# Three 256-column matmuls in place of one of 512 and one of 256 in the weight-stationary stages of a decoder layer

## Chip, cores and metric

The kernel runs on one core of one Trainium2 chip. The metric is the device time of one execution in microseconds; the kernel before takes 1761.91 us, the median of three runs (1760.35 to 1762.4).

## What is computed

One decoder layer for 256 tokens of width 2048, all in float32. Cut to what matters:

```
u  = x @ w_in + b_in                      # x: 256 x 2048, twelve column groups
mq, mk: causal convolution over 4 tokens, then SiLU      (16 blocks of 128 columns)
rq, rk: rotary phase                                     (16 blocks)
ga, gb: merge gates, sigmoid                             (32 blocks)
ya = headnorm(mlstm(mq, mk, mv)) * sigmoid(mo) @ w_branch_m   (16 blocks)
yb = headnorm(retention(rq, rk, rv)) * silu(rg) @ w_branch_r  (16 blocks)
y  = (sigmoid(ga) * ya + sigmoid(gb) * yb) @ w_out + b_out
x1 = layer_norm(alpha * x + y)
out = layer_norm(alpha * x1 + relu(x1 @ w1 + b1)**2 @ w2 + b2)   # w1: 2048 x 8192, 60 of 64 blocks
```

The products need more accuracy than one pass of the fast 32-bit matmul format gives, so each operand is split into a high and a low part, and a product is the sum of three: high times high, high times low, and low times high.

## The kernel before, in words

The weights are one stream of 608 groups of 128 x 1024 numbers. SyncE loads a group into a ring of four raw buffers (line 96). ScalarE rounds it to its high part `whi` (line 111), and VectorE subtracts to get the low part `wlo` (line 112). Three pairs of `whi` and `wlo` form the ring that TensorE reads; `next_w()` hands out the groups in order.

The projections are of two kinds, which alternate along the program.

*x-stationary* stages (`x_stationary`, lines 164 to 166) load 128 tokens of the activations into the array and stream 512 weight columns past them, three matmuls of 512 columns for each token half and each block of 128 input features.

*weight-stationary* stages (`w_stationary`, lines 145 and 147) load 128 x 128 weights into the array and stream the 256 tokens. A **step** is one block `kb` of 128 input features, of which there are 16; a **block** is 128 output features, so it has 16 steps and takes two weight groups. The activations `src[:, kb]` hold the high part of the 256 tokens and the low part of the 256 tokens side by side, 512 columns. There are 156 blocks: 16 for the convolution, 16 for the rotary phase, 32 for the gates, 16 for each branch, and 60 in the feed-forward part (12 in its first quarter, and 16 in each other). That is 156 x 16 = 2496 steps.

In the kernel before, a step is two matmuls. The first streams all 512 columns past `whi`, so that the left half of the PSUM bank `ps_w` gathers high times high, and the right half gathers the activations' low part times `whi`. The second streams the 256 high columns past `wlo` and adds to the left half. When the block ends, its consumer has two partial sums to add: ScalarE copies the right half to a tile `t` in SBUF, and VectorE adds it to the left half. There are four PSUM buffers for these sums.

Between steps, `step()` lets a background list of small work go on: the attention-like heads (`m_head`, `r_head`) and transposes (`to_pair`). The heads call `exact` (lines 375 to 377), which is also a run of three matmuls per term; in `r_head` these have 256 columns each, and each has its own weights. A scheduler fixes the order of instructions on each engine when the program is built; an engine runs its list in order.

Of the kernel before, what the change touches and what calls it, by code (L numbers as in the profile page):

```python
# [10 lines left out]
F32 = mybir.dt.float32  # L11
F32R = mybir.dt.float32r
I32 = mybir.dt.int32
AF = mybir.ActivationFunctionType
OP = mybir.AluOpType
PSUM = bass.MemoryType.PSUM

P = 128
T = 256
D = 2048  # L20
KB = D // P
# [13 lines left out]
C_BIN, C_CW, C_CB, C_MG, C_RG, C_BF, C_INVF, C_SIGN, C_LG, C_LB, NCOL = 0, 64, 128, 144, 160, 176, 240, 241, 242, 258, 274  # L35
# [4 lines left out]
def layer_kernel(ctx: ExitStack, tc: tile.TileContext, xT, x, pos, wp, wg, cols, rows, b_in, b_ff1, gbias,  # L40
                 cst, decay, sel, out):
    nc = tc.nc
    V, S, TE, G = nc.vector, nc.scalar, nc.tensor, nc.gpsimd
# [5 lines left out]
    wk = ctx.enter_context(tc.tile_pool(name="wk", bufs=2))  # L49
    sm = ctx.enter_context(tc.tile_pool(name="sm", bufs=4))  # L50
    pmm = ctx.enter_context(tc.tile_pool(name="pmm", bufs=4, space=PSUM))
    pat = ctx.enter_context(tc.tile_pool(name="pat", bufs=4, space=PSUM))

    def big(name):
        return s16.tile([P, 4096], F32, tag="s16", name=name)

    def pair(name):
        return t32.tile([P, KB, 2, T], F32R, tag="t32", name=name)

# [1 line left out]
    NG = wp.shape[0]  # L61
    RAW_B, HL_B = 4, 3
    raws, parts, place = {}, {}, {}
# [55 lines left out]
    def step():  # L119
        while bg:  # L120
            try:
                next(bg[0])
                return
            except StopIteration:
                bg.pop(0)
# [5 lines left out]
    def next_w():  # L131
        g = state["use"]
        split_until(g + HL_B)
        state["use"] += 1
        return parts.pop(g)

    def w_stationary(src, n_blocks, consume):
        for blk in range(n_blocks):
            ps = pmm.tile([P, 512], F32, tag="mm", name="ps_w")
            for g in range(KB // 8):  # L140
                hi, lo = next_w()
                for j in range(8):
                    kb = g * 8 + j
                    c = slice(j * P, (j + 1) * P)
                    TE.matmul(ps, hi[:, c], src[:, kb].rearrange("p a t -> p (a t)"),  # L145
                              start=kb == 0, stop=False)
                    TE.matmul(ps[:, :T], lo[:, c], src[:, kb, 0], start=False, stop=kb == KB - 1)  # L147
                if g == 0:
                    step()
            consume(blk, ps)  # L150
            step()
# [46 lines left out]
        return ([(g, h) for h in range(2) for g in range(HOLD)],  # L198
                [(g, h) for g in range(HOLD, n) for h in range(2)])

# [1 line left out]
    xraw = big("xraw").rearrange("p (k t) -> p k t", k=KB)  # L202
    xs = pair("xs")
    warm = cp.tile([P, 1], F32, name="warm")
# [8 lines left out]
    col = cp.tile([P, NCOL], F32, name="col")  # L213
# [16 lines left out]
    def rows_bc(dst, i):  # L230
        nc.sync.dma_start(dst, bass.AP(tensor=rows.tensor, offset=rows.offset + i * D, ap=[[0, P], [1, D]]))

# [1 line left out]
    ex = cp.tile([P, MH, 384], F32, name="ex")  # L234
    em = cp.tile([P, 2, MH], F32, name="em")
    cos_t = cp.tile([P, T], F32, name="cos_t")
# [119 lines left out]
        yield  # L356
        V.tensor_scalar(sin_t, sin_t, col[:, C_SIGN:C_SIGN + 1], None, OP.mult)

# [1 line left out]
    def rstd_of(dst, var, n):  # L360
        v = sm.tile([P, n], F32, tag=f"ve{n}", name="ve")
        V.tensor_scalar(v, var, EPS, None, OP.add)
# [119 lines left out]
                V.scalar_tensor_tensor(dst[:, eb + i, 1], t, g, dst[:, eb + i, 0].bitcast(F32),  # L482
                                       OP.mult, OP.subtract)

# [1 line left out]
    def halves(t):  # L486
        return t.rearrange("p (a b) -> p a b", a=2)

# [29 lines left out]
    mqk = big("mqk").rearrange("p (k t) -> p k t", k=16)  # L518

    def conv_silu(blk, ps):  # L520
        t = wk.tile([P, T], F32, tag="t1", name="t1")
        S.activation(t, ps[:, T:], AF.Copy)
        zp = wk.tile([P, T + 4], F32, tag="zp", name="zp")
        V.memset(zp[:, 0:4], 0.0)
        V.scalar_tensor_tensor(zp[:, 4:], ps[:, :T], col[:, C_BIN + blk:C_BIN + blk + 1], t, OP.add, OP.add)
        y = wk.tile([P, T], F32, tag="y", name="y")
        V.tensor_scalar(y, zp[:, 1:1 + T], col[:, C_CW + blk:C_CW + blk + 1],
                        col[:, C_CB + blk:C_CB + blk + 1], OP.mult, OP.add)
        for k in range(1, CONV_K):
            c = C_CW + 16 * k + blk  # L530
            V.scalar_tensor_tensor(y, zp[:, 1 + k:1 + k + T], col[:, c:c + 1], y, OP.mult, OP.add)
        sg = wk.tile([P, T], F32, tag="sg", name="sg")
        S.activation(sg, y, AF.Sigmoid)
        V.scalar_tensor_tensor(mqk[:, blk], y, MDQK ** -0.5 if blk < 8 else 1.0, sg, OP.mult, OP.mult)
# [10 lines left out]

    x_stationary(xs, KB, 4, mo_chunk)

# [1 line left out]
    hmT = []  # L549
    rqk = big("rqk").rearrange("p (k t) -> p k t", k=16)  # L550

    def rotary(blk, ps):
        t = wk.tile([P, T], F32, tag="t1", name="t1")
        S.activation(t, ps[:, T:], AF.Copy)
        z = wk.tile([P, T], F32, tag="y", name="y")
        V.scalar_tensor_tensor(z, ps[:, :T], col[:, C_BIN + 16 + blk:C_BIN + 17 + blk], t, OP.add, OP.add)
        w = wk.tile([P, T], F32, tag="sg", name="sg")
        S.copy(w[0:64], z[64:128])
        S.copy(w[64:128], z[0:64])
        V.tensor_tensor(z, z, cos_t, OP.mult)  # L560
        V.tensor_tensor(w, w, sin_t, OP.mult)
        V.tensor_tensor(rqk[:, blk], z, w, OP.add)
        if blk == 3:
            bg.append(to_pair(mo_t, hmT, C_MG, 0, 16))
# [12 lines left out]

    x_stationary(xs, KB, 4, rg_chunk)

# [1 line left out]
    def gate(dst, c0):  # L581
        def consume(blk, ps):
            t = wk.tile([P, T], F32, tag="t1", name="t1")
            S.activation(t, ps[:, T:], AF.Copy)
            V.tensor_tensor(t, ps[:, :T], t, OP.add)
            S.activation(dst[:, blk], t, AF.Sigmoid, bias=col[:, c0 + blk:c0 + blk + 1])
        return consume

    drain_bg()
    sga = big("sga").rearrange("p (k t) -> p k t", k=16)  # L590
    w_stationary(xs, 16, gate(sga, C_BIN + 32))
    sgb = big("sgb").rearrange("p (k t) -> p k t", k=16)
    w_stationary(xs, 16, gate(sgb, C_BIN + 48))

# [1 line left out]
    hrT = []  # L596

    def branch_m(blk, ps):
        t = wk.tile([P, T], F32, tag="t1", name="t1")
        S.activation(t, ps[:, T:], AF.Copy)  # L600
        V.tensor_tensor(t, ps[:, :T], t, OP.add)
        V.tensor_tensor(sga[:, blk], sga[:, blk], t, OP.mult)

    bg.append(to_pair(rg_t, hrT, C_RG, 0, 16))
    w_stationary(hmT[0], 16, branch_m)
# [6 lines left out]
    mgT = pair("mgT")  # L612

    def branch_r(blk, ps):
        t = wk.tile([P, T], F32, tag="t1", name="t1")
        S.activation(t, ps[:, T:], AF.Copy)
        V.tensor_tensor(t, ps[:, :T], t, OP.add)
        y = wk.tile([P, T], F32, tag="y", name="y")
        V.tensor_tensor(y, sgb[:, blk], t, OP.mult)
        V.tensor_tensor(y, sga[:, blk], y, OP.add)  # L620
        S.copy(mgT[:, blk, 0], y)
        V.tensor_tensor(mgT[:, blk, 1], y, mgT[:, blk, 0].bitcast(F32), OP.subtract)
        if blk in (4, 8):
            half = blk // 4 - 1
            V.scalar_tensor_tensor(xr[:, half], xr[:, half], ALPHA, bob, OP.mult, OP.add)

    w_stationary(hrT[0], 16, branch_r)

# [1 line left out]
    hold(G_OUT + 24 + 8 - HOLD, [(s16, 2), (s16, 2), (s16, 2)])  # L630
    hold(G_FF, [(s16, 2), (s16, 2), (s16, 2)])
    st1 = sm.tile([P, 2, 4, 6], F32, tag="st1", name="st1", bufs=2)
# [48 lines left out]

    x_split(mgT, *late(KB), first_norm)

# [1 line left out]
    hT = pair("hT")  # L685
    brow = wk.tile([P, 512], F32, tag="brow", name="brow")
    nc.sync.dma_start(brow, bass.AP(tensor=b_ff1.tensor, offset=b_ff1.offset, ap=[[0, P], [1, 512]]))
# [18 lines left out]
    b2 = big("b2")[:, 0:D]  # L706
# [14 lines left out]
    for q in range(4):  # L721
        if q:
            hT = pair("hT")

        def up(blk, ps, q=q, hT=hT):
            blk += 4 if q == 0 else 0
            t = wk.tile([P, T], F32, tag="t1", name="t1")
            S.activation(t, ps[:, T:], AF.Copy)
            V.tensor_tensor(t, ps[:, :T], t, OP.add)
            c = C_BF + q * 16 + blk  # L730
            rl = wk.tile([P, T], F32, tag="sg", name="sg")
            S.activation(rl, t, AF.Relu, bias=col[:, c:c + 1])
            y = wk.tile([P, T], F32, tag="y", name="y")
            V.tensor_tensor(y, rl, rl, OP.mult)
            S.copy(hT[:, blk, 0], y)
            V.tensor_tensor(hT[:, blk, 1], y, hT[:, blk, 0].bitcast(F32), OP.subtract)
            if q == 0 and blk in (9, 10, 11, 12):
                skip_rows(blk - 9)

        w_stationary(x1T, 16 if q else 12, up)  # L740
        if q == 3:
            hold(G_FF + 4 * 64 - HOLD, [(s16, 2), (t32, 4)])

        def down(c, ps, q=q):
            for half in range(2):
                if q < 3:
                    o = xr[:, half, c * 512:(c + 1) * 512]
                    V.tensor_tensor(o, ps[half], o, OP.add)
                else:
                    add_half(c, half, ps[half], st2)  # L750

        x_stationary(hT, KB, 4 if q < 3 else 3, down)
# [16 lines left out]
    x_split(hT, *late(KB), second_norm)  # L769


# [1 line left out]
def _stat(w):  # L773
    k, n = w.shape
    return w.reshape(k // P // 8, 8, P, n // P, P).transpose(3, 0, 2, 1, 4).reshape(-1, P, GW)
# [27 lines left out]
def _lay_out(i):  # L803
    w_in, b_in = np.asarray(i["w_in"])[0], np.asarray(i["b_in"])[0]
    w1, w2 = np.asarray(i["w_ff1"])[0], np.asarray(i["w_ff2"])[0]
    c = lambda o, n: w_in[:, o:o + n]  # noqa: E731
    parts = [_move(c(O_MV, D)), _stat(c(O_MQ, D)), _move(c(O_MO, D)), _stat(c(O_RQ, D)), _move(c(O_RV, D)),
             _move(c(O_RG, D)), _stat(c(O_GA, 2 * D)), _stat(np.asarray(i["w_branch_m"])[0]),
             _stat(np.asarray(i["w_branch_r"])[0]), _move(np.asarray(i["w_out"])[0])]
# [4 lines left out]
    wp = np.concatenate(parts, axis=0)  # L814
    x = np.asarray(i["x"])[0]
    cst, dec, sel, fc = _constants()
    b2 = lambda v: np.asarray(v).reshape(-1, P).T  # noqa: E731
    cols = np.concatenate([
        b2(b_in[O_MQ:O_MQ + D]), b2(b_in[O_RQ:O_RQ + D]), b2(b_in[O_GA:O_GA + 2 * D]),
        *[b2(np.asarray(i["m_conv_w"])[0][k]) for k in range(CONV_K)], b2(np.asarray(i["m_conv_b"])[0]),  # L820
# [23 lines left out]
```

## Time and profile before

| | before |
|---|---|
| median of three runs | 1761.91 us |
| span of the profiled execution, first to last instruction | 1760.6 us |
| TensorE (PE) busy | 1740.9 us, 99%, 8882 matmuls and 8882 weight loads |
| VectorE (DVE) busy | 1111.0 us, 63% |
| ScalarE (ACT) busy | 840.7 us, 48% |
| granted TensorE clock | 0.998 of full speed |

The profiled execution's span lies 1.3 us under the median of the timed runs; that difference is taken as what lies around the span. Matmuls overlap in the pipeline, so that a row's duration is longer than the time it takes from the stream. What a matmul costs is the distance from its start to the start of the next one, its **pitch** in what follows.

### The profile page before, as it was taken

The page shows a single profiled execution, that of the slowest core. Times are in us where ns is not written, and L with a number is a line of the kernel's source. Part 1 is how long each engine was busy: PE and PEld are TensorE (multiplying, and loading weights), DVE is VectorE, ACT ScalarE, POOL GpSimd, SP SyncE. Part 2 cuts the span into 40 slices and gives each one's busy share as a digit, 9 for nine tenths or more (in the row PEclk, how much of TensorE's full clock was granted, in tenths as well). Part 3 has the DMA queues.
Part 4 walks back from the last instruction along what each step waited for, and adds up shares of the span by engine and source line. Part 5 has one row for each costly group of instructions (what it writes and reads, how often), then busy time and mean ns, then how long its engine had stood idle before and what let it go on. Part 6 is the DMA issues. An engine that isn't in the chain of part 4 may idle for free.

```text
span 1760.6 us, 23131 instructions
## 1 busy us (share of the span) xinstructions
PE 1740.9 (99%) x8882; PEld 1475.3 (84%) x8882; DVE 1111.0 (63%) x1535; ACT 840.7 (48%) x1144; POOL 19.7 (1%) x24
## 2 busy tenths in 40 slices
PE   8999999999999999999999999999999999999997
PEld 6888888888888888888888878888888888888885
DVE  5788766875566645466666578655665566556656
ACT  5454444654444544554444465534553455345532
POOL 0000000000000000000000000000000000000001
PEclk9999999999999999999999999999999999999999
DMA  8565545456665456555555557555555555555553
GB/s 288 177 205 188 194 166 167 168 191 203 205 206 187 163 183 238 184 193 189 188 186 189 199 186 280 192 192 192 184 188 194 191 189 187 195 191 183 189 193 130
DMA packets 96439, 339.44 MB, mean 193 GB/s; under 512 B 10820, under 2 KB 12868, under 8 KB 95304
## 3 DMA queue, kind: packets, MB, share of 16 engines
q1 hardware_dynamic: 96328, 337.97, 56.7%
q8 instruction: 69, 1.13, 0.2%
q14 instruction: 42, 0.34, 0.1%
HBM read 335.83 MB, written 2.10 MB: 192 GB/s over the span
## 4 chain that ended last, share of the span: by engine, by line
PE 58%; issue 40%; DVE 1%; POOL 0%; ACT 0%; DMA 0%; SPq 0%; POOLq 0%; ACTq 0%
PE ps_w L145 20%; PE ps_w L147 10%; PE ps_x L164 8%; PE ps_x L165 8%; PE ps_x L166 8%; PE tp L475 0%; PE n L375 0%; PE ps_x L187 0%; PE ps_x L186 0%; PE ps_x L185 0%; PE n L376 0%; PE n L377 0%; PE gp L247 0%; PE sp L382 0%; DVE xr L766 0%
## 5 line engine op out<-in xcount | busy, mean ns | idle before, releaser
L112 DVE TENSOR_TENSOR wlo<-raw,whi 128x1024 fp32r<-128x1024 f32 (+1 forms) x593 | 722.7, 1219 | 545.3 <-ACT whi L111 541.8
L111 ACT CAST whi<-raw 128x1024 fp32r<-128x1024 f32 (+1 forms) x593 | 619.8, 1045 | 706.1 <-PE ps_x L165 377.2
L145 PE MATMUL ps_w<-xs,whi 128*128 128x512 f32 x1024 | 363.4, 399 | 0.0
L145 PE MATMUL ps_w<-x1T,whi 128*128 128x512 f32 x960 | 338.1, 397 | 0.0
L147 PE MATMUL ps_w<-xs,wlo 128*128 128x256 f32 x1024 | 287.6, 281 | 0.0
L147 PE MATMUL ps_w<-x1T,wlo 128*128 128x256 f32 x960 | 269.5, 281 | 0.0
L145 PEld LDWEIGHTS ps_w<-xs,whi 128*128 128x128 f32 x1024 | 192.4, 188 | 47.0
L145 PEld LDWEIGHTS ps_w<-x1T,whi 128*128 128x128 f32 x960 | 180.2, 188 | 43.9
L164 PE MATMUL ps_x<-whi,xs 128*128 128x512 f32 x512 | 201.8, 394 | 4.9 <-ACT whi L111 4.9
L165 PE MATMUL ps_x<-whi,xs 128*128 128x512 f32 x512 | 200.6, 392 | 0.0
L166 PE MATMUL ps_x<-wlo,xs 128*128 128x512 f32 x512 | 200.1, 391 | 0.0
L147 PEld LDWEIGHTS ps_w<-xs,wlo 128*128 128x128 f32 x1024 | 193.5, 189 | 0.1
L165 PE MATMUL ps_x<-whi,hT 128*128 128x512 f32 x480 | 186.8, 389 | 0.0
L164 PE MATMUL ps_x<-whi,hT 128*128 128x512 f32 x480 | 186.8, 389 | 0.0
L166 PE MATMUL ps_x<-wlo,hT 128*128 128x512 f32 x480 | 186.7, 389 | 0.0
L145 PE MATMUL ps_w<-yT,whi 128*128 128x512 f32 x512 | 181.8, 400 | 0.0
L147 PEld LDWEIGHTS ps_w<-x1T,wlo 128*128 128x128 f32 x960 | 181.4, 189 | 0.2
L147 PE MATMUL ps_w<-yT,wlo 128*128 128x256 f32 x512 | 143.8, 281 | 0.0
L164 PEld LDWEIGHTS ps_x<-whi,xs 128*128 128x128 f32 x512 | 96.8, 189 | 25.5 <-ACT whi L111 5.0
L145 PEld LDWEIGHTS ps_w<-yT,whi 128*128 128x128 f32 x512 | 96.2, 188 | 23.5
L166 PEld LDWEIGHTS ps_x<-wlo,xs 128*128 128x128 f32 x512 | 96.8, 189 | 20.6 <-DVE wlo L112 0.2
L165 PEld LDWEIGHTS ps_x<-whi,xs 128*128 128x128 f32 x512 | 96.9, 189 | 19.7
(246 smaller groups left out, 1546.5 us busy)
## 6 DMA issues: line engine op xcount, KB each, us to landing
raw<-in_wp SPq DMA_DIRECT2D x601, 512.0 KB, 3.4
brow<-in_b_in SPq DMA_DIRECT2D x16, 256.0 KB, 4.4
gb<-in_rows SPq DMA_DIRECT2D x4, 1024.0 KB, 8.2
raw<-in_wp SPq DMA_DIRECT2D x14, 256.0 KB, 4.6
xraw<-in_xT SPq DMA_DIRECT2D x8, 256.0 KB, 6.5
xr<-in_x SPq DMA_DIRECT2D x1, 2048.0 KB
dec<-in_decay SPq DMA_DIRECT2D x8, 192.0 KB, 3.1
bob<-in_rows SPq DMA_DIRECT2D x1, 1024.0 KB, 5.4
```

Of the source, the lines that this page charges most:

```text
L111: S.copy(hi[:, c], r[:, c])
L112: V.tensor_tensor(lo[:, c], r[:, c], hi[:, c].bitcast(F32), OP.subtract)
L145: TE.matmul(ps, hi[:, c], src[:, kb].rearrange("p a t -> p (a t)"), start=kb == 0, stop=False)
L147: TE.matmul(ps[:, :T], lo[:, c], src[:, kb, 0], start=False, stop=kb == KB - 1)
L164: TE.matmul(ps[half], src[:, kb, 0, t], hi[:, w], start=first, stop=False)
L165: TE.matmul(ps[half], src[:, kb, 1, t], hi[:, w], start=False, stop=False)
L166: TE.matmul(ps[half], src[:, kb, 0, t], lo[:, w], start=False, stop=last)
```

## The change

A step of `w_stationary` becomes three matmuls of 256 columns: `whi` with the high columns, `whi` with the low columns, `wlo` with the high columns. All three add to the same 256 columns of PSUM, so the finished sum stands there when the block ends. The tile `t`, the copy to it, and the addition go away in all six consumers; ScalarE (or VectorE, in the branches) reads the sum from PSUM, and adds the bias on the way.

```diff
     def w_stationary(src, n_blocks, consume):
         for blk in range(n_blocks):
-            ps = pmm.tile([P, 512], F32, tag="mm", name="ps_w")
+            ps = pmm.tile([P, T], F32, tag="mm", name="ps_w")
...
-                    TE.matmul(ps, hi[:, c], src[:, kb].rearrange("p a t -> p (a t)"),
-                              start=kb == 0, stop=False)
-                    TE.matmul(ps[:, :T], lo[:, c], src[:, kb, 0], start=False, stop=kb == KB - 1)
+                    TE.matmul(ps, hi[:, c], src[:, kb, 0], start=kb == 0, stop=False)
+                    TE.matmul(ps, hi[:, c], src[:, kb, 1], start=False, stop=False)
+                    TE.matmul(ps, lo[:, c], src[:, kb, 0], start=False, stop=kb == KB - 1)
...
     def conv_silu(blk, ps):
-        t = wk.tile([P, T], F32, tag="t1", name="t1")
-        S.activation(t, ps[:, T:], AF.Copy)
         zp = wk.tile([P, T + 4], F32, tag="zp", name="zp")
         V.memset(zp[:, 0:4], 0.0)
-        V.scalar_tensor_tensor(zp[:, 4:], ps[:, :T], col[:, C_BIN + blk:C_BIN + blk + 1], t, OP.add, OP.add)
+        S.activation(zp[:, 4:], ps, AF.Identity, bias=col[:, C_BIN + blk:C_BIN + blk + 1])
...
         def consume(blk, ps):
-            t = wk.tile([P, T], F32, tag="t1", name="t1")
-            S.activation(t, ps[:, T:], AF.Copy)
-            V.tensor_tensor(t, ps[:, :T], t, OP.add)
-            S.activation(dst[:, blk], t, AF.Sigmoid, bias=col[:, c0 + blk:c0 + blk + 1])
+            S.activation(dst[:, blk], ps, AF.Sigmoid, bias=col[:, c0 + blk:c0 + blk + 1])
...
     def branch_m(blk, ps):
-        t = wk.tile([P, T], F32, tag="t1", name="t1")
-        S.activation(t, ps[:, T:], AF.Copy)
-        V.tensor_tensor(t, ps[:, :T], t, OP.add)
-        V.tensor_tensor(sga[:, blk], sga[:, blk], t, OP.mult)
+        V.tensor_tensor(sga[:, blk], ps, sga[:, blk], OP.mult)
...
         def up(blk, ps, q=q, hT=hT):
             blk += 4 if q == 0 else 0
-            t = wk.tile([P, T], F32, tag="t1", name="t1")
-            S.activation(t, ps[:, T:], AF.Copy)
-            V.tensor_tensor(t, ps[:, :T], t, OP.add)
             c = C_BF + q * 16 + blk
             rl = wk.tile([P, T], F32, tag="sg", name="sg")
-            S.activation(rl, t, AF.Relu, bias=col[:, c:c + 1])
+            S.activation(rl, ps, AF.Relu, bias=col[:, c:c + 1])
```

`rotary` changes as `conv_silu` does, and `branch_r` as `branch_m` does.

How the lists of the engines change is seen at two places. On TensorE, where the first weight-stationary stage (the convolution's) follows an x-stationary one, the list before reads:

```order
L166 MATMUL ps_x<-wlo,xs 128x512
L145 MATMUL ps_w<-xs,whi 128x512
L147 MATMUL ps_w<-xs,wlo 128x256
L145 MATMUL ps_w<-xs,whi 128x512
L147 MATMUL ps_w<-xs,wlo 128x256
L145 MATMUL ps_w<-xs,whi 128x512
L147 MATMUL ps_w<-xs,wlo 128x256
```

and now, with the activations `xs` streamed and `whi` or `wlo` loaded:

```order
L166 MATMUL ps_x<-wlo,xs 128x512
L145 MATMUL ps_w<-xs,whi 128x256
L146 MATMUL ps_w<-xs,whi 128x256
L147 MATMUL ps_w<-xs,wlo 128x256
L145 MATMUL ps_w<-xs,whi 128x256
L146 MATMUL ps_w<-xs,whi 128x256
L147 MATMUL ps_w<-xs,wlo 128x256
```

Three steps stood in these rows, and two stand there now; the columns streamed in a step stay 768, the matmuls go from two to three, and nothing else moves on TensorE.

On ScalarE, in the middle of the convolution's stage, the list before reads (`t` is the copied right half, `sg` the sigmoid of the convolved block, `whi` the rounding of the next weight groups):

```order
L111 CAST whi<-raw 128x1024 x2
L533 ACTIVATE sg<-y 128x256
L522 ACTIVATE t_1366<-ps_w 128x256
L111 CAST whi<-raw 128x1024 x2
L533 ACTIVATE sg<-y 128x256
L522 ACTIVATE t_1424<-ps_w 128x256
```

and now:

```order
L111 CAST whi<-raw 128x1024
L523 ACTIVATE zp<-ps_w,col 128x256
L111 CAST whi<-raw 128x1024
L531 ACTIVATE sg<-y 128x256
L111 CAST whi<-raw 128x1024
L523 ACTIVATE zp<-ps_w,col 128x256
```

The sigmoid, which waits for VectorE, has moved from behind both roundings of a block to between them; the instruction that reads the block's sum stands at the same distance in roundings as before.

## Rows read from the trace of the kernel before

**Rows 1.** The page's head, and the busy time of each engine:

```profile
span 1760.6 us, 23131 instructions
PE 1740.9 (99%) x8882; PEld 1475.3 (84%) x8882; DVE 1111.0 (63%) x1535; ACT 840.7 (48%) x1144; POOL 19.7 (1%) x24
```

**Rows 2.** Chain that ended last, shares of the span by engine:

```profile
PE 58%; issue 40%; DVE 1%; POOL 0%; ACT 0%; DMA 0%; SPq 0%; POOLq 0%; ACTq 0%
```

**Rows 3.** Waits of PE: total us, times, longest us:

```profile
PE ps_x L164 <- ACT whi L111: 4.9, 1, 4.9
PE ps_x L187 <- DVE ve L362: 1.4, 1, 1.4
PE tp L667 <- ACT xr L664: 0.5, 1, 0.5
```

**Rows 4.** PE groups by line and shape: count, busy us, mean ns, idle before:

```profile
L145 PE MATMUL ps_w<-xs,whi 128*128 128x512 f32 x1024 | 363.4, 399 | 0.0
L145 PE MATMUL ps_w<-x1T,whi 128*128 128x512 f32 x960 | 338.1, 397 | 0.0
L145 PE MATMUL ps_w<-yT,whi 128*128 128x512 f32 x512 | 181.8, 400 | 0.0
```

**Rows 5.** Busy time by engine in an x-stationary, then a weight-stationary stage:

```profile
1306.20:1393.10 86.90, 86.90 (x386) 71.97 (x385) 44.73 (x43) 34.73 (x35) 0.00 (x0) 1.00 0.57 194
1215.80:1306.10 90.30, 90.30 (x512) 78.36 (x511) 56.19 (x79) 48.35 (x77) 0.00 (x0) 1.00 0.54 187
```

**Rows 6.** Timeline of PE, three weight-stationary steps: start us, duration us:

```profile
1250.05 0.40 PE L145 MATMUL ps_w<-x1T,whi 128*128 128x512 f32 x1
1250.29 0.28 PE L147 MATMUL ps_w<-x1T,wlo 128*128 128x256 f32 x1
...
1251.11 0.40 PE L145 MATMUL ps_w<-x1T,whi 128*128 128x512 f32 x1
```

**Rows 7.** Timeline of PE, three x-stationary matmuls and the first step behind them:

```profile
102.07 0.39 PE L164 MATMUL ps_x<-whi,xs 128*128 128x512 f32 x1
...
102.75 0.39 PE L145 MATMUL ps_w<-xs,whi 128*128 128x512 f32 x1
```

**Rows 8.** Timeline of PE, a head's nine 256-column matmuls inside an x-stationary stage:

```profile
505.53 0.28 PE L375 MATMUL n<-rv,ph 128*128 128x256 f32 x1
505.65 0.28 PE L376 MATMUL n<-rv,pl 128*128 128x256 f32 x1
...
506.59 0.40 PE L164 MATMUL ps_x<-whi,xs 128*128 128x512 f32 x1
```

**Rows 9.** Timeline of the weight loads (PEld) of the same run:

```profile
505.54 0.19 PEld L376 LDWEIGHTS n<-rv,pl 128*128 128x128 f32 x1
```

**Rows 10.** Timeline of PE, the same run of a later head, inside a weight-stationary stage:

```profile
580.24 0.28 PE L377 MATMUL n<-rv,ph 128*128 128x256 f32 x1
...
581.03 0.28 PE L147 MATMUL ps_w<-xs,wlo 128*128 128x256 f32 x1
581.15 0.40 PE L145 MATMUL ps_w<-xs,whi 128*128 128x512 f32 x1
```

**Rows 11.** Timeline of PE, eleven steps in the feed-forward part's first quarter:

```profile
1090.11 0.28 PE L147 MATMUL ps_w<-x1T,wlo 128*128 128x256 f32 x1
...
1093.93 0.28 PE L147 MATMUL ps_w<-x1T,wlo 128*128 128x256 f32 x1
```

**Rows 12.** Instructions on the tile `t`: ns min/median/max, first and last start:

```profile
L728 ACT ACTIVATE t<-ps_w x60: 369/377/386, 1068.7 to 1662.3; 128x256 f32<-128x256 f32 x60
L729 DVE TENSOR_TENSOR t<-ps_w,t x60: 415/417/425, 1069.1 to 1663.6; 128x256 f32<-128x256 f32 x60
L525 DVE SCALAR_TENSOR_TENSOR zp<-ps_w,col,t x16: 475/476/479, 110.7 to 195.9; 128x256 f32<-128x256 f32 x16
```

**Rows 13.** The page's groups of the split: busy us, mean ns, idle before:

```profile
L112 DVE TENSOR_TENSOR wlo<-raw,whi 128x1024 fp32r<-128x1024 f32 (+1 forms) x593 | 722.7, 1219 | 545.3 <-ACT whi L111 541.8
L111 ACT CAST whi<-raw 128x1024 fp32r<-128x1024 f32 (+1 forms) x593 | 619.8, 1045 | 706.1 <-PE ps_x L165 377.2
```

More of the change, by code (lines that the diff above doesn't have):

```diff
@@ L552, in rotary @@
     def rotary(blk, ps):
-        t = wk.tile([P, T], F32, tag="t1", name="t1")
-        S.activation(t, ps[:, T:], AF.Copy)
         z = wk.tile([P, T], F32, tag="y", name="y")
-        V.scalar_tensor_tensor(z, ps[:, :T], col[:, C_BIN + 16 + blk:C_BIN + 17 + blk], t, OP.add, OP.add)
+        S.activation(z, ps, AF.Identity, bias=col[:, C_BIN + 16 + blk:C_BIN + 17 + blk])
         w = wk.tile([P, T], F32, tag="sg", name="sg")
@@ L614, in branch_r @@
     def branch_r(blk, ps):
-        t = wk.tile([P, T], F32, tag="t1", name="t1")
-        S.activation(t, ps[:, T:], AF.Copy)
-        V.tensor_tensor(t, ps[:, :T], t, OP.add)
         y = wk.tile([P, T], F32, tag="y", name="y")
-        V.tensor_tensor(y, sgb[:, blk], t, OP.mult)
+        V.tensor_tensor(y, ps, sgb[:, blk], OP.mult)
         V.tensor_tensor(y, sga[:, blk], y, OP.add)
@@ L726, in up @@
             blk += 4 if q == 0 else 0
-            t = wk.tile([P, T], F32, tag="t1", name="t1")
-            S.activation(t, ps[:, T:], AF.Copy)
-            V.tensor_tensor(t, ps[:, :T], t, OP.add)
             c = C_BF + q * 16 + blk
             rl = wk.tile([P, T], F32, tag="sg", name="sg")
-            S.activation(rl, t, AF.Relu, bias=col[:, c:c + 1])
+            S.activation(rl, ps, AF.Relu, bias=col[:, c:c + 1])
             y = wk.tile([P, T], F32, tag="y", name="y")
```

## The prediction

> **What bounds the kernel now.** I read four views, in this order. The page's head first: TensorE is busy 99% of a span of 1760.6 us, VectorE 63%, ScalarE 48% [rows 1]. A busy TensorE need not be a full one, so the chain that ended last comes next. It gives TensorE 58% and "issue" 40%, and nearly nothing to any other engine [rows 2]: the end is set by matmuls that follow one another, not by a wait for a consumer. The waits of TensorE agree: 4.9 us once at the start, then 1.4 and 0.5 us [rows 3], and no idle time at all ahead of the three groups of line 145 [rows 4]. So the time of a weight-stationary stage is its number of steps times the time that TensorE takes for one, and the rest of this prediction is about that time.
>
> For it I leave the durations, which overlap, and take starts. In a steady weight-stationary stage three steps take 1251.11 − 1250.05 = 1.06 us, so one takes **353.3 ns** [rows 6]; the stage's window says the same, 90.30 us for 512 matmuls, 256 steps [rows 5]. In the feed-forward part's first quarter eleven steps take 3.82 us, so one takes 347.3 ns there [rows 11]. An x-stationary matmul of 512 columns takes (102.75 − 102.07)/3 = 226.7 ns [rows 7]. Those stages are not touched by the change, and are the yardstick for what 512 columns cost.
>
> There are 1024 + 960 + 512 = 2496 steps [rows 4]. 192 of them, 12 blocks, lie in the first quarter. A nanosecond for each step is 2.5 us, or 0.14% of the time. That is the scale of everything below.
>
> **The change part by part.**
>
> *Consumers.* The copy to `t` takes 0.37 us of ScalarE, and the addition 0.42 or 0.48 us of VectorE [rows 12]. Over 156 blocks that is up to 156 × 0.377 = 59 us less on ScalarE, of which 32 copies stay (convolution and rotary turn the copy into one that adds the bias), so some 47 us; and 124 × 0.417 + 32 × 0.477 = 67 us less on VectorE. I cost this at nothing. What hides it is TensorE: it does not wait for these engines in these stages [rows 3, 4]. A gain is bounded by TensorE's waits, which lie elsewhere: the 4.9 us at the start and the 1.4 us come in front of x-stationary work. A loss would need ScalarE to be late with the roundings. They have 706.1 us of idle time in front of them, more than half of it waiting for TensorE to free a ring buffer [rows 13]. In the convolution's stage the sigmoid now stands between the two roundings of a block, so the second one waits behind it for VectorE's chain (some five operations of 0.4 to 0.5 us, and one or two `wlo` subtractions of 1.2 us, 4 to 5 us in all [rows 12, 13]); a block takes 16 × 0.353 = 5.65 us and the ring holds three groups, half a block each. I take nothing here too; if the cover were gone, sixteen blocks late by 0.5 us would be 8 us.
>
> *Matmuls.* Columns stay at 768 for each step. One more weight load and one more matmul come in: 2496 each, 28% more than the 8882 of before. Does the pair of `whi` matmuls share one load? The trace counts as many loads as matmuls [rows 1], so I take three loads for a step.
>
> What three 256-column matmuls, each with its own load, cost in a row, the trace shows in the heads' runs. In the first, which begins behind steady x-stationary work as most weight-stationary stages do, nine matmuls take 506.59 − 505.53 = 1.06 us, **117.8 ns** each [rows 8]. Their loads start with them: the load of the second starts 0.01 us after the first matmul [rows 9], so a load is hidden behind one 256-column matmul, though with nothing to spare. Three times 117.8 is 353.3 ns. That is the time of the step of before: 2304 columns take 1.06 us in both [rows 6, 8].
>
> In a later head's run, inside a weight-stationary stage, seven matmuls take 581.03 − 580.24 = 0.79 us, 112.9 ns each; by 226.7/2 it would be 113.3, so this is the yardstick's rate without any loss [rows 7, 10]. Three would be 340 ns, 13.3 less than now. But the first matmul of the stage's own operands behind it takes 0.12 us again [rows 10].
>
> So the new step has two prices from rows, 340 and 353.3 ns. I take 353.3: it is the rate on entry from x-stationary work, held for all nine matmuls, and the cheaper sequence stopped as soon as the operands of a weight-stationary stage came.
>
> *Sum.* 2304 steps at 353.3 − 353.3 = 0; the 192 of the first quarter at 353.3 − 347.3 = 6 ns more, 1.2 us; consumers 0. 1760.6 + 1.2 = 1761.8 us of span. The median lies 1.3 us above the span shown, so **1763 us**, which is no change that can be measured. Its own range is 1759 to 1767.
>
> The Trainium skill ("TensorE: Matmul & The Clock Gate", section "Back-to-back issue gap") gives a gap of N/2.4 + 2.5 ns at the full clock. That is 216 + 109 = 325 ns for the old step and 328 for the new, so 2.5 ns a step, an estimate of 6 us more. The trace does not agree with its level: 353.3 ns for the old step [rows 6].
>
> **The rivals.**
>
> *Slower: a fixed cost for each matmul.* A 512-column matmul takes 226.7 ns in an x-stationary stage, and two of 256 columns 2 × 117.8 = 235.6 [rows 7, 8]: cutting one in two costs 8.9 ns. If a weight-stationary step loses its present 353.3 − (226.7 + 117.8) = 8.8 ns for another reason, such as the roles of the two operands, then the cut adds its 8.9 on top: 362.2 ns, 2496 × 8.9 = 22 us, **1784 us**. It decides as soon as the step exceeds 354.8 ns, 0.2% of the time. For it speaks that three loads must now each hide behind a 256-column matmul; against it, that the nine matmuls of the first head carried three loads in every 353.3 ns [rows 8]. They were only nine, and a stage has 768 or more; the trace shows no longer run. The section of the Trainium skill just named is this rival's rule, a fixed part for each matmul; the trace agrees that there is one, but not with 2.5 ns.
>
> *Faster in part.* The cheaper rate [rows 10] is taken up wherever a head or a burst of transposes has broken the rhythm, and then held. Such stages are the rotary one, the gates and branches, which follow one another, and the first quarter: 16 + 64 blocks, 1280 steps at 13.3 ns, and 192 at 7.3. That is 17.0 + 1.4 = 18 us less, **1744 us**. For it: the first quarter does run at another rate, 347.3 ns, from its start's disturbance to its end [rows 11], so a rhythm once found can be kept. Against: the 0.12 us at the end of that sequence [rows 10].
>
> *Faster throughout.* The stall belongs to the mix of 512 and 256 columns, and equal matmuls run at 113.3 ns: 2304 × 13.3 + 1.4 = 32 us less, **1730 us**. Against it stand the nine matmuls at 117.8 ns [rows 8].
>
> **How the numbers follow.** No change 0.42, slower 0.23, faster in part 0.23, faster throughout 0.12. A measurement of this kernel tells 0.2%, 3.5 us, from no change (its three runs lie within 0.12%). The likeliest case is 1763. The range goes down to 1741, which takes in the partly faster case and leaves out the full one, 0.12; and up to 1781, which takes in a fixed cost of up to 8 ns a step and leaves out the rest, some 0.08.
>
> **What would show it.** In the profile after, TensorE has 11378 matmuls and as many loads. Three starts of line 145 in a row in a weight-stationary stage lie 1.06 us apart; 1.02 us would show the cheaper rate, 1.09 the fixed cost. The same window question by stage tells whether stages differ. TensorE shows no idle time ahead of the groups of `ps_w`; if it does, and ends it on line 111 or 112, the consumers' new order was wrongly costed at nothing. VectorE's busy time falls by some 67 us, ScalarE's by some 40 to 50, with no effect on the span. The prediction is wrong if the short sequences of the heads do not stand for a stage of several hundred equal matmuls, in either direction.

## The result, and the profile after

The changed kernel takes **1780.53 us** (median of 4 runs, 1780.24 to 1781.86) beside 1762.16 us for the kernel before on the same chip: a ratio of **1.0103**, 95% interval 1.0091 to 1.0116. It is slower by 18 us. (Two later executions enter no comparison: one of the kernel called e2 below, 2471.45 us, and the first of e5, 3525.67 us, which ran at half pace from end to end, though its trace lists a granted clock of 1.000, and was repeated.)

The page's head and busy times, which answer to [rows 1]:

```profile
span 1778.5 us, 27765 instructions
PE 1758.8 (99%) x11378; PEld 1609.0 (90%) x11378; DVE 1056.8 (59%) x1379; ACT 810.0 (46%) x1020; POOL 19.2 (1%) x24
```

11378 matmuls and as many loads: every matmul brings its own. VectorE has 54 us less to do and ScalarE 31 us, and the span has grown by 17.9 us all the same. The chain that ended last has not changed its kind [rows 2]:

```profile
PE 58%; issue 40%; DVE 1%; POOL 0%; DMA 0%; ACT 0%; POOLq 0%
```

Nor have the waits of TensorE (total us, times, longest us); as in [rows 3], none stands ahead of a `ps_w`:

```profile
PE ps_x L164 <- ACT whi L111: 5.3, 1, 5.3
PE ps_x L187 <- DVE ve L362: 1.4, 1, 1.4
PE tp L654 <- ACT xr L651: 0.5, 1, 0.5
```

So the 17.9 us lie in the matmuls themselves. Busy time by engine in the second quarter's two stages, the weight-stationary one first; the columns are the window, its length, then PE, PEld, DVE, ACT and POOL with their counts, the granted clock, DMA share and GB/s:

```profile
1228.50:1320.60 92.10, 92.10 (x769) 92.06 (x769) 51.56 (x64) 43.78 (x62) 0.00 (x0) 1.00 0.54 184
1320.70:1407.50 86.80, 86.80 (x385) 71.91 (x384) 44.02 (x41) 34.42 (x34) 0.00 (x0) 1.00 0.57 194
```

(A window's count takes in a matmul that hangs over its edge.) The x-stationary stage is what it was, 86.8 us beside 86.9 [rows 5]. The weight-stationary one, 768 matmuls or 256 steps, went from 90.3 to 92.1 us: 120.0 ns a matmul and 360 ns a step, at the same granted clock. The timeline of PE inside it (start us, duration us), which answers to [rows 6]:

```profile
1250.14 0.28 PE L145 MATMUL ps_w<-x1T,whi 128*128 128x256 f32 x1
1250.26 0.28 PE L146 MATMUL ps_w<-x1T,whi 128*128 128x256 f32 x1
1250.38 0.28 PE L147 MATMUL ps_w<-x1T,wlo 128*128 128x256 f32 x1
1250.50 0.28 PE L145 MATMUL ps_w<-x1T,whi 128*128 128x256 f32 x1
...
1251.10 0.28 PE L147 MATMUL ps_w<-x1T,wlo 128*128 128x256 f32 x1
```

0.12 us each, without exception, where the prediction had hoped for 0.1178. That pace holds in all weight-stationary stages, the first quarter's too:

```profile
1080.00:1140.00 60.00, 60.00 (x502) 60.00 (x501) 39.02 (x54) 29.24 (x42) 0.00 (x0) 1.00 0.61 205
```

2304 steps at 360 − 353.3 = 6.7 ns and 192 at 360 − 347.3 = 12.7 ns [rows 6, 11] are 15.4 + 2.4 = 17.8 us: the whole of the difference in the spans.

### The profile page after: what moved, and what is told of

The parts are those of the page before. It is cut to its first block, busy times and chain, and to the rows that moved or that the text cites. A ratio compares the mean times of both kernels' runs of the same rounds, so it can differ in the third digit from the quotient of the medians.

```text
span 1778.5 us, 27765 instructions
## 1 busy us (share of the span) xinstructions
PE 1758.8 (99%) x11378; PEld 1609.0 (90%) x11378; DVE 1056.8 (59%) x1379; ACT 810.0 (46%) x1020; POOL 19.2 (1%) x24
## 4 chain that ended last, share of the span: by engine, by line
PE 58%; issue 40%; DVE 1%; POOL 0%; DMA 0%; ACT 0%; POOLq 0%
PE ps_w L146 10%; PE ps_w L147 10%; PE ps_w L145 10%; PE ps_x L164 8%; PE ps_x L165 8%; PE ps_x L166 8%; PE tp L475 0%; PE ps_x L187 0%; PE ps_x L185 0%; PE ps_x L186 0%; PE n L375 0%; PE n L376 0%; PE n L377 0%; PE gp L247 0%; PE sp L382 0%
## 5 line engine op out<-in xcount | busy, mean ns | idle before, releaser
L145 PE MATMUL ps_w<-xs,whi 128*128 128x256 f32 x1024 | 290.6, 284 | 0.0
L146 PE MATMUL ps_w<-xs,whi 128*128 128x256 f32 x1024 | 289.7, 283 | 0.0
L146 PE MATMUL ps_w<-x1T,whi 128*128 128x256 f32 x960 | 271.8, 283 | 0.0
L145 PE MATMUL ps_w<-x1T,whi 128*128 128x256 f32 x960 | 271.7, 283 | 0.0
L146 PEld LDWEIGHTS ps_w<-xs,whi 128*128 128x128 f32 x1024 | 196.5, 192 | 0.1
L145 PEld LDWEIGHTS ps_w<-xs,whi 128*128 128x128 f32 x1024 | 196.5, 192 | 0.1
L145 PEld LDWEIGHTS ps_w<-x1T,whi 128*128 128x128 f32 x960 | 184.3, 192 | 0.2
L146 PEld LDWEIGHTS ps_w<-x1T,whi 128*128 128x128 f32 x960 | 184.3, 192 | 0.2
L145 PE MATMUL ps_w<-yT,whi 128*128 128x256 f32 x512 | 145.5, 284 | 0.0
```

Source lines behind the costliest of these rows:

```text
L145: TE.matmul(ps, hi[:, c], src[:, kb, 0], start=kb == 0, stop=False)
L146: TE.matmul(ps, hi[:, c], src[:, kb, 1], start=False, stop=False)
```

## The experiments

A pitch is read below as a window's length divided by its matmuls; in a window of 60 us the matmuls that hang over its edges make it up to 0.6 ns too low. e3 to e8 were executed once each, so that their whole times tell little; their stages are what is read.

### Which half of the change costs it

e1 has the three matmuls, but lets the low activations' product into the right half of the region, and keeps the old consumers. Against the kernel before:

```
-  TE.matmul(ps, hi[:, c], src[:, kb].rearrange("p a t -> p (a t)"), start=kb == 0, stop=False)
+  TE.matmul(ps[:, :T], hi[:, c], src[:, kb, 0], start=kb == 0, stop=False)
+  TE.matmul(ps[:, T:], hi[:, c], src[:, kb, 1], start=False, stop=False)
```

> Three 256-column matmuls for each step, but the low-part product goes to the right half of the bank as before, and the consumers of before copy and add. If the whole 18 us come from the matmuls: 1780 us, steps of 360 ns. If part of it comes from the consumers' new order on ScalarE: clearly under 1780, down to 1762 if all does.

Measured: 1779.89 us, ratio 1.0098 (1.0084 to 1.0112). e2 has the old matmuls and the new consumers, which read the left half alone (`consume(blk, ps[:, :T])`).

> The two matmuls of before, with the changed consumers, which read only the left half of the bank; the addition of the right half (low part of the activations times high part of the weights) is left out. If the matmuls carry the loss: 1762 us, steps of 353 ns. If the consumers carry a part of it: over 1765.

Measured: 1762.67 us, ratio 0.9999 (0.9990 to 1.0009), with VectorE at 1056.9 us and ScalarE at 810.4 us as in the changed kernel. The matmuls are the whole loss, and the 85 us of busy time taken off the two other engines are worth nothing.

### A fixed cost for each matmul, or a load that is too long?

e3 gives each stage its own number of columns n (the three matmuls of a step then take the columns `[:n]`, `[512 - n:]` and `[:n]`; the first matmul of a block keeps at least 256).

> As the changed kernel, but in all but the first of a block's 16 steps the three matmuls stream another number of columns in each stage: 288 in the convolution's, 224 and 192 in the gates', 320 and 240 in the branches', 384, 128 and 160 in the feed-forward quarters two to four; 256 stays in the rotary one and the first quarter. Tokens beyond are left out, or low-part columns taken in their place. Only the start-to-start time in each stage is read. Theory A, the load sets it: a weight load can't be ready for the next matmul sooner than 120 ns after the start of this one; then 128 to 256 columns all take 120 ns, and 288, 320 and 384 take the streaming rate of 512 columns, 0.4427 ns each: 127.5, 141.7 and 170.0. Theory B, a fixed cost of 6.7 ns for each matmul beside that rate: 63, 78, 92, 106, 113, 120, 134, 148 and 177 ns for 128, 160, 192, 224, 240, 256, 288, 320 and 384.

Windows of stages (same columns as above) with 128, 192, 240, 256, 288 and 384 columns:

```profile
1466.20:1551.90 85.70, 85.70 (x769) 85.70 (x767) 51.34 (x64) 43.68 (x62) 0.00 (x0) 1.00 0.61 197
690.00:760.00 70.00, 70.00 (x628) 70.00 (x628) 31.87 (x26) 32.33 (x40) 0.00 (x0) 1.00 0.66 227
895.00:965.00 70.00, 70.00 (x624) 70.00 (x623) 47.28 (x65) 31.46 (x40) 0.00 (x0) 1.00 0.60 196
1088.80:1158.80 70.00, 70.00 (x585) 69.94 (x584) 48.26 (x65) 33.93 (x48) 0.00 (x0) 1.00 0.66 226
103.60:205.00 101.40, 101.40 (x769) 101.40 (x768) 73.96 (x125) 47.72 (x65) 0.00 (x0) 1.00 0.51 169
1245.90:1378.90 133.00, 133.00 (x768) 132.96 (x768) 51.58 (x64) 45.33 (x62) 0.00 (x0) 1.00 0.39 128
```

The pitches are 111.6, 111.5, 112.2, 119.9, 132.0 and 173.2 ns. Half as many columns still cost 111.6: up to 240 columns something else than the stream sets the pace. PEld, busy all the time, suggests the load; narrower loads beside such short streams were not tried, so that is not shown. By the yardstick of 226.7 ns for 512 columns [rows 7] the streams of the last three would take 113.3, 127.5 and 170.0; they lose 6.6, 4.5 and 3.2 ns (and the stage with 320 columns, whose starts lie 147 ns apart, some 5). Neither theory came out: the floor is near 111.5, not 120, and the loss is no constant. It is greatest where the stream is just longer than the floor. (The Trainium skill, "TensorE: Matmul & The Clock Gate", section "LDWEIGHTS (loading the stationary operand)", gives a load columns/1.2 ns, by which an estimate for 128 columns is 107 ns; the floor of 111.6 ns lies some 4% above it.)

e4 leaves the stream alone and narrows the loads: `hi[:, c][:, :m]` into `ps[:m]`, m by stage.

> As the changed kernel, but in all but the first and last of a block's 16 steps the weight loads have fewer columns in some stages (the other output features are left out): 96 for all three in the convolution's stage, 64 in the second gate's, 32 in the second branch's; in the feed-forward quarters two to four 128, 128 and 64; 128, 64 and 64; 96, 64 and 96. All matmuls stream 256 columns. Theory A, the load sets the time: with 96 columns or fewer all fall to 113.3 ns, and in a mixed step only the matmul during which a 128-column load runs stays at 120. Theory B, a fixed cost for each matmul: 120 ns everywhere.

The stages with all loads 64, 96 and 32 wide:

```profile
700.00:750.00 50.00, 50.00 (x440) 50.00 (x439) 22.07 (x18) 22.69 (x28) 0.00 (x0) 1.00 0.58 190
110.00:190.00 80.00, 80.00 (x691) 80.00 (x690) 64.73 (x115) 42.26 (x59) 0.00 (x0) 1.00 0.57 190
860.00:940.00 80.00, 80.00 (x690) 75.25 (x689) 52.15 (x71) 34.63 (x43) 0.00 (x0) 1.00 0.58 190
```

113.6, 115.8 and 115.9 ns, beside 120.0 with loads of 128: the streams are the same, and most of the loss goes when the loads get narrower. It does not fall in step with the width, so it isn't simply the load's length. Nor does it belong to one matmul alone. Stages with loads of 128, 128 and 64 in a step, then of 128, 64 and 64:

```profile
1230.00:1300.00 70.00, 70.00 (x601) 70.00 (x600) 40.10 (x50) 34.72 (x51) 0.00 (x0) 1.00 0.59 188
1400.00:1480.00 80.00, 80.00 (x681) 80.00 (x679) 45.55 (x57) 38.89 (x56) 0.00 (x0) 1.00 0.58 187
```

They come to 116.5 and 117.5 ns in the mean, where theory A's 120.0 beside each load of 128 would give 117.8 and 115.5: the second narrow load makes it dearer. A narrow load also means a narrow output here, so e4 alone does not tell the two apart; the runs that follow, which move the streamed or the loaded tile and leave the output's width alone, speak for the load.

### What load and stream have to do with each other

They read the same memory. Three kernels move tiles there, by an unused tile of 32 bytes at the head of everything (e6), or of 32 (e7) or 64 bytes (e8) between the weights and all that follows, the activations first:

```
e6   cp.tile([P, 8], F32, name="pad")
e7   t32.tile([P, 8], F32, tag="pad", name="pad", bufs=1)
e8   t32.tile([P, 16], F32, tag="pad", name="pad", bufs=1)
```

> The changed kernel, with 32 bytes put ahead of the weight ring, so that all that follows starts 32 bytes later, on a multiple of 128 bytes. If the extra time over 113.3 ns comes from reads that straddle a line: 113 ns a matmul, 1745 to 1748 us. If it is a matter of the load beside the stream alone: 120 ns, 1780 us.

> The changed kernel, with 32 bytes put between the weight ring and the activations: weights stay where they were, activations start on a multiple of 128 bytes. If loads and streams collide by their relative place in a line: another time than 120 ns a matmul, between 113 and 127. If not: 120 ns, 1780 us.

> The same with 64 bytes. If the relative place in a line matters, another time than with 0 and 32 bytes; if not, 120 ns and 1780 us.

e6, 1779.54 us; a weight-stationary stage:

```profile
1228.50:1320.60 92.10, 92.10 (x767) 92.01 (x767) 50.87 (x63) 43.59 (x63) 0.00 (x0) 1.00 0.56 183
```

e7, 1780.32 us; the convolution's stage, then an x-stationary one:

```profile
106.20:195.70 89.50, 89.50 (x769) 89.50 (x768) 71.64 (x125) 47.77 (x65) 0.00 (x0) 1.00 0.58 192
1139.60:1229.00 89.40, 89.40 (x386) 72.00 (x385) 44.34 (x41) 34.32 (x34) 0.00 (x0) 1.00 0.56 189
```

e8, 1775.05 us; the convolution's stage, the second gate stage, an x-stationary one:

```profile
104.70:195.00 90.30, 90.30 (x768) 90.29 (x767) 71.64 (x125) 47.81 (x65) 0.00 (x0) 1.00 0.56 190
690.00:750.00 60.00, 60.00 (x532) 60.00 (x531) 26.97 (x22) 27.28 (x34) 0.00 (x0) 1.00 0.60 197
1131.70:1221.10 89.40, 89.40 (x386) 71.66 (x385) 44.34 (x41) 34.19 (x34) 0.00 (x0) 1.00 0.57 188
```

Moving everything changes nothing. Moving the activations against the weights changes every pitch: at 32 bytes 256 columns fall from 120.0 to 116.5 ns, at 64 bytes to 117.6 and, in the stages between 328 and 797 us of the span, to 113. In both, 512 columns of the x-stationary stages, where the activations are the loaded tile, rise from 226 to 232.8 ns, which takes most or all of it back; so the whole time hides what the stages show. What counts is the **distance** between the streamed and the loaded tile. In the memory map of the changed kernel, and of the one before, the streamed activations `xs`, `yT` and `x1T` and all six weight buffers leave the same remainder by 512 bytes (`xs` at 70496, the first `whi` at 45920), and the slices that a matmul takes of them begin on multiples of 512 bytes: distance 0. The heads' operands, from which the prediction took its price, do not: `rv` lies 448 bytes beyond a multiple of 512 from `ph`, since the two `zp` buffers ahead of `ph` are no multiple of 512 long.

e5 varies within a step which weights and activations meet, at distance 0: the low weights second, the high weights three times, the high activations three times, the old 512-column matmul for two steps and then two low parts ("pairs"), and an x-stationary stage cut into 256 columns.

> As the changed kernel, with one thing varied in each stage. Convolution and third feed-forward quarter: the low weights come second, so that no load repeats the one before. Second gate and fourth quarter: the third matmul takes the high weights too, so that all three loads of a step are the same (leaves out the low part of the weights). Second branch: all three stream the high columns (leaves out the activations' low part). Second quarter: the 512-column matmul of before, with the two 256-column ones of two steps behind each other (its right half is not added). Retention values, an x-stationary stage: each 512-column matmul cut into two of 256, the activations still loaded and the weights streamed. If the 120 ns come from a 128-column load that runs beside a 256-column stream, whatever the operands: 120 ns in all of these but the second quarter. If repeated loads or the one ring buffer that is read twice matter: 113 or 118 ns in the convolution's stage. If the roles of the operands matter: 113 ns in the cut x-stationary stage. The second quarter: 353 ns a step if only the mean count of 256-column matmuls matters, up to 347 to 360 otherwise.

What is read comes from a second execution of the same kernel:

> The changed kernel, whose first execution of this form ran at half the TensorE clock throughout and so told nothing; again as one look. Stages differ in the three matmuls of a step, and some leave out or change part of the sum: the conv and third up stages issue the low weights second (same sum); the second gate stage and the fourth up stage use the high weights three times; the second branch stage uses the high activations three times; the second up stage streams 512 columns twice for a pair of steps and then the two low parts; the retention values' weight-moving stage is cut from 512 to 256 columns. The rest is as changed. Theory A (the 120.0 ns come from what one matmul's stream and the next one's load touch in SBUF at the same time): 120.0 ns in the plain stages, another figure by at least 1 ns in one of the changed ones, and the cut weight-moving stage, whose loaded tile and streamed tile have changed places, still above 113.3. Theory B (a fixed cost of any 256-column matmul that follows one of its own size): 120.0 in all of them, about 117 on average in the pairs, since half of the columns come in 512. Time between 1755 and 1785 us.

The stages with the low weights second, the high weights three times, and pairs:

```profile
102.40:194.40 92.00, 92.00 (x768) 92.00 (x767) 72.56 (x125) 46.22 (x65) 0.00 (x0) 1.00 0.56 186
1587.70:1679.70 92.00, 92.00 (x768) 91.96 (x768) 51.59 (x64) 43.64 (x62) 0.00 (x0) 1.00 0.54 184
1232.30:1321.40 89.10, 89.10 (x513) 77.72 (x512) 51.55 (x64) 43.90 (x62) 0.00 (x0) 1.00 0.56 189
```

and the cut x-stationary stage, six matmuls in 0.72 us:

```profile
449.87 0.28 PE L184 MATMUL ps_x<-whi,xs 128*128 128x256 f32 x1
...
450.59 0.28 PE L184 MATMUL ps_x<-whi,xs 128*128 128x256 f32 x1
```

120 ns wherever 256 columns follow 256. Order, sameness of the operands and their roles do not matter; the cut stage rules out the rival's "roles of the two operands" for matmuls of 256 columns. Pairs cost 89.10/256 = 348.0 ns a step beside 352.7 in the same stage of before [rows 5]. Theory B fits these numbers as well as theory A, which had asked for another figure somewhere; it is e7 and e8 that speak against B.

### Distances, one after another

e9 moves the activations of the changed kernel by 128 bytes (`xs`), 192 and 256 (`yT` of the two branches) and 320 (`x1T`); e10 does the same to the kernel before:

```
+        off = {"xs": 128, "x1T": 320}.get(name, 0) // 4
+        if name == "yT":
+            off = shifts.pop(0) // 4
+        t = t32.tile([P, n + 128], F32R, tag="t32", name=name)
+        return t[:, off:off + n].rearrange("p (k a t) -> p k a t", k=KB, a=2)
```

> The changed kernel, complete, with the streamed activations moved in SBUF against the weights (whose tiles all begin on the same remainder of 512 bytes): by 128 bytes in the conv, rotary and gate stages, 192 in the first branch stage, 256 in the second, 320 in the four up stages. Moved by 32 bytes they cost 120.0 ns a matmul, by 64 bytes 113.3 to 117.7. Theory A (the remainder of the distance between streamed and loaded tile sets the price): a figure of its own for each place, the larger distances at or below 117.7; with 113.3 everywhere the time is 1780 - 7488 x 6.7 ns = 1730 us, with 117.7 everywhere 1763 us. Theory B (64 bytes was an accident of that run and 120.0 is what a matmul of 256 columns costs behind another): 120.0 in every stage and 1780 us.

(What it says of 32 bytes was misread: e7's stage window gives 116.5, not 120.0.)

> The kernel before, complete, with the same shifts of the activations (and one buffer instead of two for the t1 tile, to make room). Theory A (a step of 512 and 256 columns pays for the same meeting of stream and load, 353.3 ns where three times 113.3 would be 340.0): the step falls to between 340 and 350 ns, the time to between 1729 and 1753 us. Theory B (the 512-column matmul hides the meeting, so the place is nothing to it): 353.3 ns as before and 1761 us, within 0.2% of the kernel before.

e9, 1776.90 us, ratio 1.0078 (1.0061 to 1.0094); stages at 128 (convolution, then gates), 192, 256 and 320 bytes:

```profile
106.00:198.00 92.00, 92.00 (x769) 92.00 (x768) 71.77 (x125) 47.82 (x65) 0.00 (x0) 1.00 0.56 187
610.00:760.00 150.00, 150.00 (x1266) 150.00 (x1266) 64.68 (x53) 64.87 (x80) 0.00 (x0) 1.00 0.59 200
820.00:860.00 40.00, 40.00 (x342) 40.00 (x341) 20.13 (x21) 15.16 (x15) 0.00 (x0) 1.00 0.57 189
890.00:950.00 60.00, 60.00 (x502) 60.00 (x501) 37.98 (x54) 25.95 (x32) 0.00 (x0) 1.00 0.55 182
1231.90:1322.20 90.30, 90.30 (x768) 90.30 (x767) 51.53 (x64) 43.80 (x62) 0.00 (x0) 1.00 0.57 187
```

119.8 and 118.5, then 117.0 (a short window, so a little low), 119.5 and 117.6 ns. Larger isn't better, as theory A had guessed it would be: 128 and 256 bytes are nearly as dear as 0, and 192 and 320 cost about what 64 does in its dearer state.

e10, 1768.22 us, ratio 1.0030 (1.0019 to 1.0040); the convolution's stage and the second quarter's:

```profile
105.80:195.60 89.80, 89.80 (x513) 78.66 (x512) 77.66 (x138) 44.51 (x64) 0.00 (x0) 1.00 0.59 191
1224.50:1313.70 89.20, 89.20 (x513) 78.10 (x512) 56.18 (x79) 48.42 (x77) 0.00 (x0) 1.00 0.57 189
```

350.8 and 348.4 ns a step: the old step also pays for its place, less than theory A expected, and the x-stationary stages on `xs` took more than that back. Not every stage gains. The first quarter's, before and then in e10, where it has the same 320 bytes as the second's:

```profile
1061.10:1128.60 67.50, 67.50 (x393) 59.41 (x392) 51.53 (x76) 37.54 (x59) 0.00 (x0) 1.00 0.66 234
1068.50:1137.30 68.80, 68.80 (x393) 59.84 (x392) 51.63 (x76) 37.61 (x59) 0.00 (x0) 1.00 0.66 229
```

Its 192 steps, 347.3 ns each at distance 0 [rows 11], became dearer by 1.3 us, some 7 ns a step. So the distance does not fix the pace of the old step alone: at 0 and at 320 bytes it has two.

### The weights moved instead

e11 moves the weights, and only in the weight-stationary stages, so that `xs` keeps distance 0 where 512 columns stream against it. One buffer for the `zp` tile makes the room.

```
+    AHEAD = {(32, 64): 64, (96, 128): 192, (192, 224): 64, (224, 256): 192, (256, 288): 192, (288, 320): 320,
+             (360, 384): 448, (416, 448): 192, (480, 512): 96, (544, 576): 48}
+    def ring(g):
+        s = [(512 - a) // 4 for (m, n), a in AHEAD.items() if m <= g < n]
+        c = slice(s[0], s[0] + GW) if s else slice(0, GW)
+        return (wpool.tile([P, GW + 128], F32R, tag="whi", bufs=HL_B, name="whi")[:, c],
+                wpool.tile([P, GW + 128], F32R, tag="wlo", bufs=HL_B, name="wlo")[:, c])
```

> The changed kernel, complete, with the weights of the weight-stationary stages alone moved inside their tiles (and one buffer for the zp tile, to make room), so that the streamed activations lie so many bytes ahead of the loaded weights, beyond a multiple of 512: conv 64, rotary 192, first gate stage 64, second 192, first branch stage 192, second 320, up stages 448, 192, 96 and 48. The weight-moving stages keep their places, which the runs with moved activations did not: there 512 columns rose from 226.7 to 233 ns and ate what the 256-column matmuls gave. Theory A (the remainder to 128 bytes decides; 0 costs 120.0, 64 costs 117.7 or 113.3, 32 costs 116.7): 117.7 or 113.3 ns in the first eight stages, between 113.3 and 120 in the last two, 226.7 ns for 512 columns; with 117.7 in all 1763 us, with 113.3 in all 1730 us, so between the two, and below the kernel before unless 117.7 holds everywhere. Theory B (a low figure at 64 and 192 was the state of that execution or of its activations' place, not of the distance): 120.0 ns in most stages and 1775 to 1781 us.

Measured: **1749.32 us** (1748.28 to 1749.92), ratio **0.9924** (0.9910 to 0.9937): with the same matmuls, loads and counts of work on the other engines as the changed kernel it beats both. The head of its page, and windows of the stages at 64 (convolution), 192 (second gates), 320, 448, 192 (second quarter), 96 and 48 bytes, then an x-stationary stage:

```profile
span 1748.1 us, 27795 instructions
PE 1728.7 (99%) x11378; PEld 1578.6 (90%) x11378; DVE 1056.9 (60%) x1379; ACT 809.8 (46%) x1020; POOL 19.2 (1%) x24
...
103.50:193.80 90.30, 90.30 (x768) 90.30 (x767) 71.75 (x125) 47.76 (x65) 0.00 (x0) 1.00 0.58 190
690.00:750.00 60.00, 60.00 (x532) 60.00 (x531) 26.96 (x22) 27.35 (x34) 0.00 (x0) 1.00 0.60 194
870.00:930.00 60.00, 60.00 (x532) 60.00 (x531) 40.19 (x56) 26.93 (x33) 0.00 (x0) 1.00 0.61 194
1049.10:1115.30 66.20, 66.20 (x584) 66.12 (x583) 47.97 (x65) 33.83 (x48) 0.00 (x0) 1.00 0.69 239
1202.50:1292.80 90.30, 90.30 (x768) 90.30 (x767) 51.54 (x64) 43.73 (x62) 0.00 (x0) 1.00 0.58 187
1380.00:1472.10 92.10, 92.10 (x769) 92.08 (x768) 51.53 (x64) 43.85 (x62) 0.00 (x0) 1.00 0.56 183
1559.20:1648.60 89.40, 89.40 (x767) 89.36 (x767) 51.47 (x64) 43.79 (x62) 0.00 (x0) 1.00 0.57 189
1115.40:1202.30 86.90, 86.90 (x386) 71.97 (x385) 44.12 (x42) 34.41 (x34) 0.00 (x0) 1.00 0.60 194
```

117.6, 112.8, 112.8, 113.4, 117.6, 119.9 and 116.6 ns, and 226 ns for 512 columns as before. At 64 bytes beyond a multiple of 128 there are two steady paces, 117.6 and about 113; both occur at 192. So theory A held in the first eight stages and for 512 columns; e11 itself did not try distance 0 again, but its stage at 96 bytes, 119.9, speaks against the longer weight buffers as the cause of the gain, and e6 and e9 have 118.5 to 120.0 at multiples of 128. Against the changed kernel the span falls by 1778.5 − 1748.1 = 30.4 us.

## Why the prediction was right, and where it was wrong

**The bound, and the consumers at nothing: right.** e2 shows it with 0.9999. The two groups of the split had more idle time ahead of them than before [rows 13], not less:

```profile
L112 DVE TENSOR_TENSOR wlo<-raw,whi 128x1024 fp32r<-128x1024 f32 (+1 forms) x593 | 722.6, 1219 | 612.9 <-ACT whi L111 608.0 <-PE gp L247 2.4
L111 ACT CAST whi<-raw 128x1024 fp32r<-128x1024 f32 (+1 forms) x593 | 620.2, 1046 | 807.0 <-PE ps_x L165 389.4 <-PE ps_w L146 260.9 <-issue 129.2
```

The cover that hid the convolution's new order was never used up. The relief in busy time came to 54 and 31 us instead of 67 and 40 to 50. Added up instruction by instruction it is what was forecast: VectorE's durations sum to 1164.0 us before and 1097.5 after, 66.5 less, and ScalarE's to 887.2 and 840.6, 46.6 less. Instructions of one engine overlap in the trace, and busy time counts the overlap once.

**Three loads for a step: right**, 11378 matmuls and loads.

**The price of three 256-column matmuls: wrong, and this is the step that failed.** "I take 353.3: it is the rate on entry from x-stationary work, held for all nine matmuls." Measured are 360.0 ns in every stage. The nine matmuls [rows 8] were a true sample of something else: their operands lie at another distance from each other than a stage's, and e7, e8 and e11 show that the distance moves this price between some 340 and 360 ns, with the same matmuls. No run moved the heads' operands by themselves; their two prices, 117.8 and 113 ns, are those that stages show at 64 and 192 bytes, and a stage at their 448 bytes ran at 113.4. The second reason given there, that the cheaper sequence stopped as soon as a stage's operands came [rows 10], was the right thing to look at. It was read as a rhythm that broke, when it pointed to another price for these operands. In the changed kernel too the heads keep their 113 to 118 ns, the later ones amid a stage at 120.0.

**The slower rival: right in its direction and nearly in its size**, 360.0 beside 362.2 ns and 1780.5 beside 1784 us; it had a chance of 0.23. Its cause is another. A fixed part of each matmul would stand at any number of columns and any place; e3 finds 6.6, 4.5 and 3.2 ns at 256, 288 and 384 columns, e4 takes most of it away with narrower loads, and at 64 and 192 bytes it is gone where the pace is 113. (The same page of the Trainium skill, section "Back-to-back issue gap", gives for the isolated gap of one matmul N/2.4 + 2.5 ns, by which an estimate for 256 columns is 109; the least steady pitch measured here is 113, so no run reaches it.)

**The faster rivals: their pace exists**, 113 ns, and it is kept for hundreds of microseconds once found, as the second of them said; but at distance 0 no stage with full loads found it.

The range, 1741 to 1781, held the result by half a microsecond, because it reached towards the slower rival, whose cause was not the one at work; that it held is luck. The likeliest range, 1759 to 1767, did not.

**Open.** Which reads of the memory collide, and whether they do, no run shows: only that the distance and the load's width move the price. What chooses between 117.6 and 113 at the same distance is open too (a lesser split shows in e7, where at 32 bytes the second branch stage ran at 117.4 and the convolution's at 116.5); in e8 the pace changed at about 328 us, behind a run of transposes, and fell back at 797, where two starts lay 0.29 us apart. The kernel before with its weights moved as in e11 wasn't tried, so how much of e11's gain needs the change is not known; the old step's least is 347.3 ns in the kernel before [rows 11] and 348.4 in e10, where the new one has some 340 to 353 at its better places.

## What to carry to other kernels

A matmul's price taken from another place in the same trace can fail, as it did here, when the operands are alike in shape but lie otherwise in memory: compare the tiles' addresses before you carry a row over. Where TensorE never waits and a stage still runs some per cent above its columns, try moving the loaded tiles against the streamed ones, here by 64 bytes, look at each stage's window, and expect other stages that share a tile to lose what this one gains. Work taken off engines that nobody waits for is worth nothing, 85 us of busy time here.

## What was not expected of the hardware

- Distance between the streamed and the loaded tile, for 256 columns with loads of 128: 120.0 ns at 0, 118.5 to 119.8 at 128 and 119.5 at 256 bytes; about 113 or 117.6 at 64 and 192; 117.6 at 320 in e9 and 112.8 in e11; 116.5 at 32, 116.6 at 48, 119.9 at 96. For 512 columns 226 at 0 and 232.8 where the loaded tile lies 32 or 64 bytes ahead: the best place for one form is not that for the other.
- A matmul of 128, 192 or 240 columns costs 111.5 to 112.2 ns, whatever its size, with a load of 128 columns for each (e3).
